# Gate logits out of the value projection, one value product over four query blocks, and a new order for the five stages

## The chip, the cores and the metric

One core of a Trainium2 chip runs the whole program. The metric is device time in microseconds, lower is better: the median of 3 runs before is 1630.82 us (1628.48 to 1631.11). Engines by their short names: PE multiplies matrices (PEld is its weight load), DVE and ACT work on vectors, POOL is the slow general engine, SP only issues DMAs.

## The reference

Three residual layers on a sequence of 512 tokens, width 1024, in fp32. First a gated delta-rule mixer (8 heads of 128, in chunks, with a triangular solve) and a SwiGLU FFN (2816 wide); then a forgetting attention and a second FFN; then a block with two attentions side by side (a sparse one, "A", that keeps 128 keys per query chosen by an indexer, and a dense one, "B", causal in chunks of 64). What the change touches:

```python
def shared_kv(x, kv_norm, w_kv, b_forget):
    kvf = rms_norm(x, kv_norm) @ w_kv              # 1024 x (1024 keys, 1024 values, 16 gates)
    ...
    f_logit = kvf[..., 2 * FOX_WIDTH:] + b_forget  # one gate logit per token and head
    log_f_cum = jnp.cumsum(jax.nn.log_sigmoid(f_logit), axis=1).transpose(0, 2, 1)
    return k, v, log_f_cum

def forgetting_attention_mixer(h, w_q, w_o, k, v, log_f_cum):
    for blk in range(t_len // 128):                # four query blocks, keys up to their own end
        s = q_blk @ k[:e].T * scale + log_f_cum[q] - log_f_cum[keys]
        p = softmax(where(mask, s, -inf))
        outs.append(p @ v[:e])
    return concat(outs) @ w_o
```

## The kernel before, in words

Activations lie transposed: 8 tiles of 128 features x 512 tokens. Every fp32 operand of a large product is split into a high and a low part (`fp32r`), and a product is three matmuls, high x high, high x low, low x high (`mm3`). Weights come by DMA on SP, 128 x 1024 at a time; the high part is a cast on ACT or DVE, the low part is a second cast of the negated high part, to which a DMA on POOL adds the weight again, or a subtraction on DVE or POOL (`lows`, `weight`).

`fm_tile` makes one output tile of 128 features x 512 tokens (weights stand, activations move, 24 matmuls of 512 columns); `tm_group` makes a token-major product: 4 banks, one per block of 128 tokens, n weight columns moving, weight units of 128 x 1024 in turn. The value projection of the forgetting attention ("fox") is two such groups of 512 columns, 8 heads each (`values_of`).

The forget gates' logits come from `small_proj`: 16 columns, high and low parts side by side in a stationary tile padded with zeros, 16 matmuls of 512 columns, then transposed to tokens; then the log-sigmoid as a chain of small DVE steps, a scan over tokens on DVE, and transposes back. The first scores need its result (`gates`, `cq`).

`attend` is one head of any of the three attentions. For each of four query blocks: scores into a bank, softmax on DVE and ACT, transposition on PE, then the transposed probabilities are copied to their high part and subtracted into the low part. Two query blocks share one pair of tiles; as soon as both are there, each key block's values (high and low side by side, stationary) meet the high and the low part: 4 and 8 matmuls for the two pairs of query blocks.

The output projection of a mixer is halved over its input: `out_half` multiplies the first four of eight head pairs while the other heads still run; `out_proj` adds the second four, for tokens 0 to 255 and then 256 to 511, so that the norm after it (`add_normed`) starts on the first half.

The order of instructions is not that of the code. `Program.record` lists operations; `schedule` replays them on a model of the engines' queues and issues whatever can start first, the lowest key among equals. `SHIFTS` move the keys of large products back, `SELECT_SHIFT`, `SUMS_SHIFT`, `START_SHIFT` those of some other work; `WINDOWS` say how far ahead of the oldest open operation it may go; `DEAR` sets what it adds to an engine's end when an operation may go on several engines; `cost`, `timed`, `lag` and `LATE` are its durations and delays. `GDN_ORDER`, `FOX_ORDER` and `B2_ORDER` are the order in which the parts are listed: in fox V are value groups, K key projections, H a pair of heads, O the first half of the output projection; in the last block S are the selections of A (a chain of DVE maxima), B and A head pairs.

In the first stage (`gdn`), `inverses` solves four heads' triangular blocks together: blocks go through DRAM to 64 partitions, 30 dependent pairs of DVE steps follow, and the result goes back through DRAM; `doubled` then finishes it with chains of small products and copies.

Of the kernel before, what the change touches and what calls it, by code (L numbers as in the profile page):

```python
# [16 lines left out]
T = 512  # L17
NT = 4
# [23 lines left out]
SUMS_SHIFT = 53  # L42
START_SHIFT = 133
# [3 lines left out]
MARGIN, LATE, SLOW = 100, 400, 1.04  # L47
# [126 lines left out]
class Program:  # L174
# [166 lines left out]
    def schedule(self):  # L341
# [27 lines left out]
        def ready(i):  # L369
# [214 lines left out]
class Net:  # L584
# [154 lines left out]
    def fm_tile(self, out, w, xs, cols=FULL):  # L739

        nk = len(xs)
        with self.later(self.shift):
            for k in range(nk):
                a = (w[0][:, k * 128:(k + 1) * 128], w[1][:, k * 128:(k + 1) * 128])
                b = (xs[k][0][:, cols], xs[k][1][:, cols])
                self.mm3(out, a, b, k == 0, k == nk - 1)
# [124 lines left out]
    def out_proj(self, w, o, f, x, post, pre, dst):  # L871
# [14 lines left out]
    def run(self):  # L886
# [7 lines left out]
        for layer, (mix, nxt, w) in enumerate((("gdn", "fox", "gdn_w_out"), ("fox", "b2", "fox_w_o"))):  # L894
# [8 lines left out]
            with self.after(f[0]) if mix in st else nullcontext():  # L903
                x = self.loaded(src)
# [179 lines left out]
    def gdn(self, y, w_out):  # L1084
# [82 lines left out]
        def conv_silu(m, ps):  # L1167
# [7 lines left out]
            th, s = self.t(), self.t()  # L1175
# [35 lines left out]
        def keys(h):  # L1211
            s = conv_silu(8 + h, proj(8 + h))
# [6 lines left out]
            kds[h] = self.t()  # L1219
# [164 lines left out]
        for step in GDN_ORDER.split():  # L1384
# [11 lines left out]
            else:  # L1396
                f = self.out_half(w_out, [out[h] for h in range(G4)])
# [54 lines left out]
    def attend(self, passes, bias, vhl, out, row=None):  # L1452
# [4 lines left out]
        po = self.bank()  # L1457
        for p in range(2):
            ph, pl = (self.t(512 * (p + 1), F32R) for _ in range(2))
            for j in range(2):  # L1460
# [21 lines left out]
                src = pt.rearrange("p (k q) -> p k q", q=128)  # L1482
                dh, dl = (t.rearrange("p (k j q) -> p k j q", j=2, q=128)[:, :qb + 1, j] for t in (ph, pl))
                self.copy(dh, src)
                V.tensor_sub(dl, src, dh.bitcast(F32))
            last = 2 * p + 1
            for kb in range(last + 1):
# [3 lines left out]
                PE.matmul(po[:, q], vhl(kb), pl[:, c], start=False, stop=(kb == last))  # L1491
        lo = self.t(T)
# [11 lines left out]
    def fox(self, y, x, w_out):  # L1504
# [11 lines left out]
        f = self.small_proj(d["w_f"], H, xs)  # L1516
        tokens = lambda: self.t(NT * H).rearrange("p (n h) -> p n h", n=NT)
        ps, ls, w2, c, z = self.bank(), tokens(), tokens(), self.t(p=H), self.t(p=H)
        for n in range(NT):
            PE.transpose(ps[:, n * H:(n + 1) * H], f[:, n * 128:(n + 1) * 128], self.ident[0:H, 0:H])  # L1520
        V.tensor_tensor(ls, ps[:, :NT * H].rearrange("p (n h) -> p n h", n=NT),
                        y.rc[:, :, None].to_broadcast([128, NT, H]), op=OP.mult)
        V.tensor_tensor(ls, ls, bf[:, None, :].to_broadcast([128, NT, H]), op=OP.add)
        self.log1p_exp_neg_abs(w2, ls, tokens)
        V.scalar_tensor_tensor(ls, ls, 0.0, w2, op0=OP.min, op1=OP.subtract)
        ps = self.bank()
        for n in range(NT):
            PE.transpose(ps[0:H, n * 128:(n + 1) * 128], ls[:, n], self.ident)
        V.memset(z, 0.0)
        V.tensor_tensor_scan(c, ps[0:H], z, 0.0, op0=OP.add, op1=OP.add)  # L1530
        cq = self.t(NT * H)
        ps = self.bank()
        for n in range(NT):
            PE.transpose(ps[:, n * H:(n + 1) * H], c[:, n * 128:(n + 1) * 128], self.ident[0:H, 0:H])
        V.tensor_copy(cq, ps[:, :NT * H])

        gates = self.t(T, F32R, p=48)
        V.memset(gates.bitcast(F32), 0.0)
        self.split(gates[0:H], gates[32:32 + H], c, -1.0)


        vt = [self.value_tiles() for _ in range(2)]
# [479 lines left out]
```

## Time and profile before

| | before |
|---|---|
| median of 3 runs | 1630.82 us |
| profiled execution | 1631.0 us, span 1629.3 us |
| PE busy | 1599.5 us, 98% |
| PE weight loads busy | 1422.7 us, 87% |
| DVE busy | 1293.1 us, 79% |
| ACT busy | 1056.7 us, 65% |
| POOL busy | 477.8 us, 29% |
| read from memory | 258 MB |

The span runs from the first to the last instruction; a little of the execution lies around it. PE's busy time counts matmuls by modelled ends, and neighbours overlap, so what a matmul costs in a stream is the distance between starts. Nearly all instructions carry one line (552, where the planner issues them), so groups are told by tile: `wide` are tiles of 1024 columns (weights, values, probabilities), `big` of 512, `s` small ones, `psum` the banks. In a PE row the moving operand stands first, the stationary one second.

### The profile page before, as it was taken

Reading aid. Unit: us, or ns where it says so; the run is one execution under the profiler, and the core shown is the slowest. Engines: PE = TensorE matmul, PEld = TensorE weight load, DVE = VectorE, ACT = ScalarE, POOL = GpSimd, SP = SyncE. Lnnn points to the kernel's source line nnn. Section 1 sums busy time; section 2 is a strip of 40 time slices with the busy share of each in tenths; the row PEclk is TensorE's granted clock in tenths of the full one; section 3 lists DMA queues with packets and bytes.
Section 4 is the critical chain, followed back from the end, with each engine's and each line's share of the span. In section 5 each row is a group of like instructions: output and inputs, shape, how many; then the busy total and the mean of one; then the engine's idle time right before and its main releaser. Section 6 shows DMA issues by size and latency. Waiting matters only on the chain.

```text
span 1629.3 us, 28818 instructions
## 1 busy us (share of the span) xinstructions
PE 1599.5 (98%) x10184; PEld 1422.7 (87%) x10184; DVE 1293.1 (79%) x3055; ACT 1056.7 (65%) x2096; POOL 477.8 (29%) x490
## 2 busy tenths in 40 slices
PE   8999999999999999999999999999999999999998
PEld 6888888998998989888878999999989889888777
DVE  7976986799785848686969699776858669999795
ACT  8716645585654635556869686655646679796794
POOL 2502411223331433213343123322315222304610
PEclk9998999999999999999999999999999999999999
DMA  9837448367796887974355757896969983439722
GB/s 289 232 53 189 115 85 243 95 153 183 189 239 142 217 170 194 282 195 123 92 117 119 181 143 186 188 231 153 228 149 259 253 195 63 130 98 208 184 56 65
DMA packets 114512, 272.31 MB, mean 167 GB/s; under 512 B 25240, under 2 KB 30104, under 8 KB 114368
## 3 DMA queue, kind: packets, MB, share of 16 engines
q0 software_dynamic: 38128, 108.05, 37.9%
q1 hardware_dynamic: 76240, 162.42, 30.1%
q8 instruction: 80, 1.31, 0.3%
q14 instruction: 64, 0.52, 0.1%
HBM read 258.29 MB, written 12.08 MB: 166 GB/s over the span
## 4 chain that ended last, share of the span: by engine, by line
PE 79%; DVE 10%; ACT 4%; DMA 2%; issue 2%; POOL 1%; SPq 0%; DVEq 0%; POOLq 0%; ACTq 0%
PE psum L552 79%; DVE big L552 8%; ACT big L552 2%; DVE wide L552 2%; ACT wide L552 2%; DMA wide<-in_w_ffn_in_dram 1%; DVE s L552 1%; DMA big<-scratch_rows 0%; SPq L552 0%; POOL big L552 0%; ACT s L552 0%; DMA wide<-in_w_gdn_dram 0%; DMA big<-in_xT_dram 0%; DMA scratch_blocks_t<-wide 0%; POOL wide L552 0%
## 5 line engine op out<-in xcount | busy, mean ns | idle before, releaser
L552 PE MATMUL psum<-big,wide 128*128 128x256 f32 (+1 forms) x7264 | 1224.8, 325 | 14.4 <-ACT big L552 8.5
L552 PEld LDWEIGHTS psum<-big,wide 128*128 128x128 f32 x7264 | 1036.8, 189 | 124.1 <-ACT big L552 10.2
L552 DVE TENSOR_TENSOR big<-psum,big 128x256 f32<-128x256 f32 (+5 forms) x550 | 254.9, 477 | 145.6 <-PE psum L552 135.3
L552 ACT CAST wide<-wide 128x1024 fp32r<-128x1024 f32 (+4 forms) x303 | 281.0, 940 | 114.1 <-PE psum L552 67.6
L552 ACT ACTIVATE big<-big 128x256 f32<-128x256 f32 (+4 forms) x335 | 170.6, 523 | 135.8 <-DVE big L552 130.1
L552 ACT ACTIVATE wide<-wide 128x1024 fp32r<-128x1024 f32 (+4 forms) x217 | 193.7, 901 | 72.4 <-PE psum L552 53.8
L552 DVE TENSOR_TENSOR big<-big,big 128x256 f32<-128x256 f32 (+3 forms) x391 | 221.4, 581 | 21.4 <-ACT big L552 17.5
L552 PE MATMUL psum<-wide,big 128*128 128x512 f32 (+2 forms) x924 | 206.5, 372 | 1.6 <-ACT big L552 1.6
L552 DVE TENSOR_TENSOR wide<-wide,wide 128x512 f32<-128x512 f32 (+2 forms) x181 | 175.4, 976 | 33.3 <-PE psum L552 28.6
L552 PEld LDWEIGHTS psum<-wide,big 128*128 128x128 f32 x924 | 157.8, 188 | 29.7 <-ACT big L552 2.0
L552 ACT COPY big<-psum 128x512 f32<-128x512 f32 (+7 forms) x188 | 84.1, 456 | 119.0 <-PE psum L552 117.0
L552 POOL DMA_DIRECT2D wide<-in_w_ffn_in_dram x88 | 78.5, 896 | 226.6 <-ACT wide L552 196.9
L552 ACT ACTIVATE big<-big,s 128x256 f32<-128x256 f32 (+3 forms) x227 | 119.9, 557 | 10.6 <-DVE s L552 10.2
L552 DVE SCALAR_TENSOR_TENSOR big<-big,big 128x512 f32<-128x512 f32 (+3 forms) x153 | 111.0, 728 | 15.5 <-ACT big L552 11.7
L552 POOL TENSOR_TENSOR s<-s,half 128x4 f32<-128x4 f32 (+2 forms) x50 | 64.3, 1286 | 187.0 <-DVE s L552 186.9
L552 PE MATMUL psum<-big,big 128*128 128x128 f32 (+13 forms) x672 | 111.8, 297 | 4.0 <-DVE big L552 1.7
L552 PEld LDWEIGHTS psum<-big,big 128*128 128x128 f32 (+6 forms) x672 | 88.1, 183 | 13.9 <-DVE big L552 2.6
L552 PE MATMUL psum<-ident,big 128*128 128x128 f32 (+2 forms) x564 | 93.4, 273 | 4.1 <-DVE big L552 1.7
L552 POOL DMA_DIRECT2D wide<-in_w_ffn_out_dram x64 | 56.6, 899 | 135.5 <-ACT wide L552 125.9
L552 POOL TENSOR_TENSOR wide<-wide,wide 128x512 f32<-128x512 f32 (+1 forms) x40 | 68.4, 1709 | 74.0 <-DVE wide L552 26.7
L552 PEld LDWEIGHTS psum<-ident,big 128*128 128x128 f32 (+2 forms) x564 | 67.3, 141 | 19.5 <-DVE big L552 3.4
L552 POOL TENSOR_TENSOR big<-big,big 64x512 fp32r<-64x512 f32 (+3 forms) x44 | 55.4, 1264 | 86.1 <-ACT big L552 43.7
(131 smaller groups left out, 1383.3 us busy)
## 6 DMA issues: line engine op xcount, KB each, us to landing
wide<-in_w_ffn_in_dram SPq DMA_DIRECT2D x88, 512.0 KB
wide<-in_w_ffn_in_dram POOLq DMA_DIRECT2D x48, 512.0 KB, 5.8
wide<-in_w_gdn_dram SPq DMA_DIRECT2D x31, 512.0 KB
wide<-in_w_ffn_out_dram SPq DMA_DIRECT2D x32, 384.0 KB
wide<-in_w_ffn_out_dram POOLq DMA_DIRECT2D x32, 384.0 KB, 7.4
wide<-in_w_gdn_dram POOLq DMA_DIRECT2D x22, 512.0 KB, 7.7
wide<-in_w_ffn_in_dram POOLq DMA_DIRECT2D x40, 256.0 KB, 6.1
wide<-in_w_ffn_out_dram SPq DMA_DIRECT2D x32, 320.0 KB
```

Of the source, the lines that this page charges most:

```text
L552: getattr(eng[o.eng], fn)(*(real(a) for a in args), **{k: real(a) for k, a in kw.items()})
```

## The change

- **Gates.** `small_proj` and its transposes are gone from fox (gdn keeps its own). The values' weights are packed as three groups of 5, 5 and 6 heads (`VALUES`), and the gates' 16 columns stand behind the first group's 320. V0's evacuation writes the logits by token, scaled, with the bias. `forget`, the same chain as before, follows V0 in the list.
- **Value products.** With `joint`, `attend` waits for all four query blocks; the probabilities of a key block then lie side by side in one of two tile pairs, and each key block has one matmul over all query blocks that see it, for each part: 512, 384, 256 and 128 columns. `JOINT` turns it on in fox and in A, not in B.
- **Late half.** With `LATE_OUT` = 2 in fox, the last four of eight output tiles get only tokens 0 to 255 in `out_half`; the other 256 are accumulated in `out_proj` ahead of the second half's own terms, with the weights loaded once more. In gdn it is 0.
- **Order.** Constants of the planner, three lists, and four of its prices change.
- `WIDE_KEYS` is empty, so the keys' tiles of gdn stay as they are.

```diff
-SHIFTS = {"gdn": 103, "ffn0": 286, "fox": 0, "ffn1": 95, "b2": 261}
-DEAR = {"gdn": {"DVE": 1050, "ACT": -450, "POOL": 1350},
-        "ffn0": {"DVE": 1200, "ACT": -350, "POOL": 1250},
-        "fox": {"DVE": 450, "ACT": -200, "POOL": 1000},
-        "ffn1": {"DVE": 1700, "ACT": -100, "POOL": 1800},
-        "b2": {"DVE": 450, "ACT": -300, "POOL": 600}}
-WINDOWS = {"gdn": 861, "ffn0": 1118, "fox": 2257, "ffn1": 762, "b2": 938}
-GDN_ORDER = ("K1 K2 K0 K3 P0 P2 I0 K4 D0 P1 D1 R0 R1 D3 P3 R3 K7 D2 K5 K6 I1 R2 P5 O0 D4 D5 D7 "
+SHIFTS = {"gdn": 121, "ffn0": 321, "fox": 21, "ffn1": 87, "b2": 278}
+DEAR = {"gdn": {"DVE": 1050, "ACT": -350, "POOL": 1350},
+        "ffn0": {"DVE": 850, "ACT": 150, "POOL": 1500},
+        "fox": {"DVE": 450, "ACT": 0, "POOL": 1000},
+        "ffn1": {"DVE": 1900, "ACT": -100, "POOL": 1600},
+        "b2": {"DVE": 550, "ACT": -500, "POOL": 550}}
+WINDOWS = {"gdn": 861, "ffn0": 885, "fox": 810, "ffn1": 930, "b2": 978}
+GDN_ORDER = ("K1 K2 K0 K3 P0 P2 I0 K4 D0 P1 D1 R0 R1 D3 P3 R3 K7 D2 K5 K6 I1 D5 R2 P5 O0 D4 D7 "
              "D6 P7 P4 P6 R4 R5 R7 R6")
-FOX_ORDER = "V0 K012 K4 H2 K6 H1 K3 H3 K7 H0 V1 H6 K5 H4 H7 H5 O"
-B2_ORDER = "B1 B3 S3 B2 S2 S1 B0 v k q o A1 A0 A2 A3"
-SELECT_SHIFT = 1156
-SUMS_SHIFT = 53
-START_SHIFT = 133
+VALUES = (0, 5, 10, 16)
+FOX_ORDER = "K012 V0 K4 V1 H2 K6 H1 K3 K7 H3 H0 V2 H6 K5 H4 H7 H5 O"
+B2_ORDER = "B1 B3 B0 S3 B2 S2 v k q S1 o A1 A0 A2 A3"
+SELECT_SHIFT = 1314
+JOINT = (True, False, True)
+LATE_OUT = (0, 2)
+SUMS_SHIFT = 50
+START_SHIFT = 226
-MARGIN, LATE, SLOW = 100, 400, 1.04
+MARGIN, LATE, SLOW = 100, 200, 1.04
...
         dur, size = self.cost(eng, fn, args, kw)
+        if not size and eng != "PE" and args[0].shape[0] <= 64 and dur > 300:
+            dur += 90
...
             if args[1].dt == F32R:
-                return 2.5 + max(0.8 * m, n / 2.25), 0
+                return 4.2 + max(0.8 * m, n / 2.25), 0
...
                 if q == "POOL" and o.size:
-                    o.est[q] += 220
+                    o.est[q] += 400
...
-    def out_half(self, w, o):
+    def out_half(self, w, o, late):
         f = [self.t() for _ in range(KD)]
-        self.half_product(w, o, slice(0, 512), lambda m, ps: self.copy(f[m], ps))
-        return f
+        first = KD - 2 * late
+        for m in range(0, KD, 2):
+            cols = FULL if m < first else HALVES[0]
+            for i, parts in enumerate(self.weight_pair(w, m, slice(0, 512))):
+                bank = self.bank()[:, :cols.stop]
+                self.fm_tile(bank, parts, o, cols)
+                self.copy(f[m + i][:, cols], bank)
+        return f, o, first
...
+        w4 = sum((self.weight_pair(w, m, slice(0, 512)) for m in range(first, KD, 2)), [])
         for cols in HALVES:
             acc = self.t(256)
             for m in range(KD):
                 bank = self.bank()[:, :256]
-                self.fm_tile(bank, ws[m], o, cols)
-                self.V.tensor_add(f[m][:, cols], bank, f[m][:, cols])
+                if m >= first and cols is HALVES[1]:
+                    self.fm_tile(bank, w4[m - first], o4, cols, stop=False)
+                    self.fm_tile(bank, ws[m], o, cols, start=False)
+                    self.copy(f[m][:, cols], bank)
+                else:
+                    self.fm_tile(bank, ws[m], o, cols)
+                    self.V.tensor_add(f[m][:, cols], bank, f[m][:, cols])
...
                 src = pt.rearrange("p (k q) -> p k q", q=128)
+                if joint:
+                    for a, b in ((0, min(qb + 1, 2)), (2, qb + 1)):
+                        if a < b:
...
+                            self.copy(dh, src[:, a:b])
+                            V.tensor_sub(dl, src[:, a:b], dh.bitcast(F32))
+                    continue
...
+        if joint:
+            for kb in range(NT):
+                q, c = slice(kb * 128, 512), slice((0, 512, 0, 256)[kb], (512, 896, 256, 384)[kb])
+                for part in (ph, pl):
+                    PE.matmul(po[:, q], vhl(kb), part[kb // 2][:, c], start=(kb == 0 and part is ph),
+                              stop=(kb == NT - 1 and part is pl))
...
-        f = self.small_proj(d["w_f"], H, xs)
...
+        def values_of(i):
+            def evac(tb, ps):
...
+                if i == 0:
+                    V.scalar_tensor_tensor(ls[:, tb], ps[:, n - H:], y.rc[:, tb:tb + 1], bf, op0=OP.mult, op1=OP.add)
+            n = (VALUES[i + 1] - VALUES[i]) * 64 + (H if i == 0 else 0)
+            self.tm_group([d[f"w_v{i}"][j] for j in range(4)], n, xs, evac)
...
+                if step == "V0":
+                    forget()
```

## Rows read from the trace of the kernel before

**Rows 1.** The page: busy us (share), instructions; granted clock in 40 slices.
```profile
PE 1599.5 (98%) x10184; PEld 1422.7 (87%) x10184; DVE 1293.1 (79%) x3055; ACT 1056.7 (65%) x2096; POOL 477.8 (29%) x490
...
PEclk9998999999999999999999999999999999999999
```

**Rows 2.** PE in order of time: start us, us, operation, out<-in, count.
```profile
689.67 7.12 PE L552 MATMUL psum<-wide,big 128*128 128x512 f32 x30
696.62 0.50 PE L552 MATMUL psum<-ones,big 128*128 128x1 f32 x4
...
894.67 0.92 PE L552 MATMUL psum<-wide,wide 128*128 128x256 f32 x7
895.43 0.30 PE L552 MATMUL psum<-ident,big 128*128 128x128 f32 x1
...
952.58 14.05 PE L552 MATMUL psum<-big,wide 128*128 128x256 f32 x117
966.47 0.50 PE L552 MATMUL psum<-ones,big 128*128 128x1 f32 x4
```

**Rows 3.** Windows: us, busy us (x) by PE, PEld, DVE, ACT, POOL; clock, DMA.
```profile
750.00:840.00 90.00, 89.91 (x495) 75.84 (x495) 70.59 (x244) 70.76 (x167) 31.37 (x32) 1.00 0.45 106
840.00:900.00 60.00, 57.18 (x330) 47.09 (x329) 57.78 (x227) 54.73 (x136) 20.80 (x17) 1.00 0.44 105
1540.00:1612.00 72.00, 68.59 (x404) 57.03 (x404) 65.90 (x183) 61.81 (x155) 15.84 (x12) 1.00 0.25 49
```

**Rows 4.** DVE groups by shape, windows 840 to 900 and 1540 to 1612: softmax rows.
```profile
L552 DVE CUSTOM_DVE_ANT_0 big<-psum,big 128x512 f32<-128x512 f32 x8 | 5.4, 676 | 0.0
...
L552 DVE CUSTOM_DVE_ANT_0 big<-psum,big 128x512 f32<-128x512 f32 x8 | 5.4, 679 | 0.0
```

**Rows 5.** PE and ACT in order of time [idle before], and windows, near the first inverse.
```profile
126.96 0.69 PE L552 MATMUL psum<-ident,big 128*128 128x128 f32 x2 [1.23 <-ACT big L552]
...
122.89 0.37 ACT L552 COPY big<-psum 96x256 f32<-96x256 f32 x1 [31.81 <-PE psum L552]
...
122.00:129.00 7.00, 4.89 (x40) 4.01 (x40) 4.60 (x7) 5.05 (x10) 0.57 (x1) 0.73 0.99 331
129.00:139.00 10.00, 9.62 (x55) 9.37 (x55) 5.35 (x12) 4.57 (x18) 3.48 (x4) 0.51 0.73 146
```

**Rows 6.** PE in order of time, at the start of ffn1.
```profile
973.10 2.79 PE L552 MATMUL psum<-big,wide 128*128 128x256 f32 x19 [0.63 <-DVE big L552]
976.99 13.23 PE L552 MATMUL psum<-big,wide 128*128 128x256 f32 x104 [1.09 <-ACT big L552]
```

**Rows 7.** PE in order of time: the gates' logits turned, the first scores.
```profile
719.22 0.42 PE L552 MATMUL psum<-ident,big 16*128 16x16 f32 x4
...
747.91 2.06 PE L552 MATMUL psum<-big,big 66*128 66x128 f32 x12
```

**Rows 8.** Groups by shape, whole span: busy us, mean ns | idle before us.
```profile
L552 DVE TENSOR_TENSOR wide<-psum,wide 128x512 fp32r<-128x512 f32 x32 | 22.0, 687 | 3.8 <-ACT wide L552 3.2
L552 DVE TENSOR_TENSOR wide<-psum,wide 128x384 fp32r<-128x384 f32 x32 | 17.6, 549 | 1.1 <-PE psum L552 0.5 <-ACT wide L552 0.2
L552 DVE TENSOR_TENSOR big<-psum,big 128x256 fp32r<-128x256 f32 x32 | 13.3, 417 | 0.3
L552 DVE TENSOR_TENSOR big<-psum,big 128x128 fp32r<-128x128 f32 x32 | 9.0, 283 | 0.2
...
L552 ACT CAST wide<-wide 128x1024 fp32r<-128x1024 f32 x203 | 210.4, 1046 | 78.6 <-PE psum L552 49.5 <-DVE wide L552 19.3 <-issue 6.5
L552 ACT CAST wide<-psum 128x512 fp32r<-128x512 f32 x30 | 17.3, 578 | 2.9 <-PE psum L552 2.8
L552 ACT CAST wide<-psum 128x384 fp32r<-128x384 f32 x31 | 14.8, 477 | 0.9 <-PE psum L552 0.6
L552 ACT CAST big<-psum 128x256 fp32r<-128x256 f32 x31 | 11.4, 366 | 0.1
L552 ACT CAST big<-psum 128x128 fp32r<-128x128 f32 x29 | 7.6, 262 | 0.3
```

More of the change, by code (lines that the diff above doesn't have):

```diff
@@ L736, in weight_pair, with fm_tile @@
         return [(hi[:, c], lo[:, c]) for c in (slice(0, 512), slice(512, 1024))]
-    def fm_tile(self, out, w, xs, cols=FULL):
+    def fm_tile(self, out, w, xs, cols=FULL, start=True, stop=True):
         nk = len(xs)
@@ L745, in fm_tile @@
                 b = (xs[k][0][:, cols], xs[k][1][:, cols])
-                self.mm3(out, a, b, k == 0, k == nk - 1)
+                self.mm3(out, a, b, start and k == 0, stop and k == nk - 1)
     def fm_phase(self, items, nk_cols, xs, evac, head=False, tail=False):
@@ L902, in run @@
             dst = d[f"x{layer}"] if nxt in st else d["out"]
-            with self.after(f[0]) if mix in st else nullcontext():
+            with self.after(f[0][0]) if mix in st else nullcontext():
                 x = self.loaded(src)
@@ L1211, in keys @@
         def keys(h):
-            s = conv_silu(8 + h, proj(8 + h))
+            both = self.t(1024) if h in WIDE_KEYS else None
+            s = conv_silu(8 + h, proj(8 + h), None if both is None else both[:, :512])
             ps = turned(s)
@@ L1396, in gdn @@
             else:
-                f = self.out_half(w_out, [out[h] for h in range(G4)])
+                f = self.out_half(w_out, [out[h] for h in range(G4)], LATE_OUT[0])
         return [out[h] for h in range(G4, H)], f
@@ L1450, in value_tiles, with attend @@
         return [self.t(1024, F32R).rearrange("p (h c) -> p h c", c=128) for _ in range(NT)]
-    def attend(self, passes, bias, vhl, out, row=None):
+    def attend(self, passes, bias, vhl, out, row=None, joint=False):
         V, A, PE = self.V, self.A, self.PE
         po = self.bank()
+        if joint:
+            ph, pl = ((self.t(1024, F32R), self.t(384, F32R)) for _ in range(2))
         for p in range(2):
-            ph, pl = (self.t(512 * (p + 1), F32R) for _ in range(2))
+            if not joint:
+                ph, pl = (self.t(512 * (p + 1), F32R) for _ in range(2))
             for j in range(2):
@@ L1485, in attend @@
                 V.tensor_sub(dl, src, dh.bitcast(F32))
+            if joint:
+                continue
             last = 2 * p + 1
@@ L1514, in fox @@
                         fill=NEG, base=0, channel_multiplier=1)
-        f = self.small_proj(d["w_f"], H, xs)
+        vt = [self.value_tiles() for _ in range(2)]
         tokens = lambda: self.t(NT * H).rearrange("p (n h) -> p n h", n=NT)
[L1518 to L1542, printed above, removed]
-        def values_of(half):
-            self.tm_group([d["w_v"][4 * half + i] for i in range(4)], 512, xs,
-                          lambda tb, ps: self.values(vt[half][tb], ps.rearrange("p (h c) -> p h c", c=64),
-                                                     y.rc[:, tb:tb + 1]))
+        ls, cq, gates = tokens(), self.t(NT * H), self.t(T, F32R, p=48)
@@ new lines, in values_of @@
+        def values_of(i):
+            def evac(tb, ps):
+                for half in range(2):
+                    lo, hi = max(VALUES[i], 8 * half), min(VALUES[i + 1], 8 * half + 8)
+                    if lo < hi:
+                        src = ps[:, (lo - VALUES[i]) * 64:(hi - VALUES[i]) * 64]
+                        self.values(vt[half][tb][:, lo - 8 * half:hi - 8 * half],
+                                    src.rearrange("p (h c) -> p h c", c=64), y.rc[:, tb:tb + 1])
+                if i == 0:
+                    V.scalar_tensor_tensor(ls[:, tb], ps[:, n - H:], y.rc[:, tb:tb + 1], bf, op0=OP.mult, op1=OP.add)
+            n = (VALUES[i + 1] - VALUES[i]) * 64 + (H if i == 0 else 0)
+            self.tm_group([d[f"w_v{i}"][j] for j in range(4)], n, xs, evac)
@@ new lines, in forget @@
+        def forget():
+            w2, c, z = tokens(), self.t(p=H), self.t(p=H)
+            self.log1p_exp_neg_abs(w2, ls, tokens)
+            V.scalar_tensor_tensor(ls, ls, 0.0, w2, op0=OP.min, op1=OP.subtract)
+            ps = self.bank()
+            for n in range(NT):
+                PE.transpose(ps[0:H, n * 128:(n + 1) * 128], ls[:, n], self.ident)
+            V.memset(z, 0.0)
+            V.tensor_tensor_scan(c, ps[0:H], z, 0.0, op0=OP.add, op1=OP.add)
+            ps = self.bank()
+            for n in range(NT):
+                PE.transpose(ps[:, n * H:(n + 1) * H], c[:, n * 128:(n + 1) * 128], self.ident[0:H, 0:H])
+            V.tensor_copy(cq, ps[:, :NT * H])
+            V.memset(gates.bitcast(F32), 0.0)
+            self.split(gates[0:H], gates[32:32 + H], c, -1.0)
@@ L1602, in fox @@
             else:
-                f = self.out_half(w_out, self.parts([o.pop(m) for m in range(4)]))
+                f = self.out_half(w_out, self.parts([o.pop(m) for m in range(4)]), LATE_OUT[1])
         return self.parts([o[m] for m in range(4, KD)]), f
@@ L1954, in pack @@
     out["w_k"] = pack_fm(w[:, :1024])
-    out["w_v"] = pack_tm(w[:, 1024:2048], 512)
-    out["w_f"] = np.ascontiguousarray(w[:, 2048:].reshape(KD, 128, 16).transpose(1, 0, 2))
+    for n in range(3):
+        cols = w[:, 1024 + 64 * VALUES[n]:1024 + 64 * VALUES[n + 1]]
+        if n == 0:
+            cols = np.concatenate([cols, w[:, 2048:]], 1)
+        out[f"w_v{n}"] = pack_tm(cols, cols.shape[1])
     out["b_forget"] = i["b_forget"].reshape(1, 16)
```

21 lines of the change are left out of this document (14 added, 7 removed).

## The prediction

> **What bounds the kernel now.** I read the page first: busy time by engine, then the slices and the granted clock. PE is busy for 1599.5 of 1629.3 us and its clock row is full but for the fourth slice [rows 1]. So nearly every microsecond is PE's, and an edit counts by how much PE work it takes away and by what it does to the few places where PE stands. Next I read PE in order of time, to price a matmul by the distance from one group's start to the next (the printed durations overlap). 30 matmuls of 512 columns take 696.62 - 689.67 = 6.95 us, 231.7 ns each; 117 of 256 columns take 966.47 - 952.58 = 13.89 us, 118.7 ns each; the seven last of a value product, five of 256 and two of 128 columns, take 895.43 - 894.67 = 0.76 us, so (760 - 5 x 118.7) / 2 = 83 ns for 128 columns [rows 2]. Halving 256 columns thus saves only a third. The places where PE stands come from the windows. In 840 to 900 us PE idles 2.8 us while DVE is 57.78 of 60 busy and ACT 54.73; in 1540 to 1612 PE idles 3.4 us with DVE at 65.90 and ACT at 61.81 of 72 [rows 3]. These are the stretches of the attention heads: the softmax rows of 512 columns count eight of fox's sixteen in the first and all eight of attention A in the second [rows 4]. The third place is the first triangular inverse, near 122 us: PE waits 1.23 us among small products, ACT has stood for 31.81 us, and the clock, full before, averages 0.73 in 122 to 129 and 0.51 in 129 to 139, so PE is at the lower level, 1.2 GHz [rows 5]. The fourth is the start of ffn1, with waits of 0.63 and 1.09 us [rows 6].
>
> **Part 1, the gates' logits.** Removed: the separate projection, 16 matmuls of 512 columns and 4 small transposes: 16 x 231.7 = 3.71 us, and 0.42 us [rows 2, 7]. Changed: the value projections were 2 groups x 96 matmuls of 512 columns and become 3 groups x 96 of 336 (16 of them the gates), 320 and 384 columns. No row has these widths; on the line between 118.7 and 231.7 ns (0.441 ns a column) they cost 154.0, 146.9 and 175.2. Before 192 x 231.7 = 44.49 us, after 96 x 476.1 = 45.71: +1.22. Sum of part 1: -3.71 - 0.42 + 1.22 = -2.91 us, all on PE, in a stretch where PE is the bound. Its bounds: 1040 columns at the 512's own 0.4525 ns each cost 96 x 470.6 = 45.18, +0.69, so -3.44; at the 256's 0.4637 ns, 46.29, +1.80, so -2.33. The weights now come in 12 units instead of 8: 4 more SP and POOL issues, and 4 more pairs of casts, which are narrower each; I cost them at nothing, since ACT is 70.76 of 90 us busy while PE has no gap [rows 3]; uncovered, four pairs of casts at 1.05 us each [rows 8] would be 8.4 us of ACT, less what the narrower ones give back. The wait that is added: the log-sigmoid chain now follows the last unit of V0, which stands behind K0 to K2. DVE's small operations queue behind it, and the first scores wait for its end. Before, the logits were turned at 719.22 and the first scores ran at 747.91 [rows 7], 29 us that PE filled with projections; after, K4 and V1 stand in that gap. I take 0, with up to 4 us if V0 drains late.
>
> **Part 2, one value product over four query blocks.** It applies to fox (16 heads) and attention A (8), not to B. A head had 8 matmuls of 256 and 4 of 128 columns: 8 x 118.7 + 4 x 83 = 1282 ns. It gets two each of 512, 384, 256 and 128: 2 x (231.7 + 175.2 + 118.7 + 83) = 1217 ns. The columns are the same, 2560; what goes is 4 matmuls, 65 ns a head, 1.6 us for 24 heads. On the other side the transposed probabilities now lie in two tiles, so that query blocks 2 and 3 are copied and subtracted in two pieces. DVE: 549 becomes 417 + 283, 687 becomes 2 x 417, +298 ns a head; the copies, nearly all on ACT: 477 becomes 366 + 262, 578 becomes 2 x 366, +305 ns [rows 8]. For 24 heads that is 7.2 us of DVE and 7.3 of ACT. Where PE is the bound it is free. In the two stretches of [rows 3] DVE is the bound: 8 x 0.298 = 2.4 us each. I take it as exposed in A, where all heads lie in one stretch and nothing stands behind, and as hidden in fox, where heads can start into the emptier 750 to 840 us (DVE 70.59 of 90). Part 2: -1.6 + 2.4 = +0.8 us, between -1.6 (all hidden) and -1.6 + 16 x 0.603 = +8.0 (both engines exposed one after the other in both).
>
> The Trainium skill's page "TensorE: Matmul & The Clock Gate", section "Back-to-back issue gap", gives columns over 2.4 GHz and 2.5 ns for a matmul alone, so 55.8 ns for 128 columns, and 81 ns measured where each brings its weight load. By the first a head would go from 1097 to 1087 ns and this part would save PE 0.24 us instead of 1.6, which speaks against it (the whole sum would be 1625.2); the trace, with 83 ns [rows 2], agrees with the second.
>
> **Part 3, the late half of fox's output projection.** Four of its eight output tiles are computed in the first pass for the first 256 tokens only; the other 256 are made later, in the bank of the second pass. 48 matmuls of 512 become 96 of 256: 48 x (237.4 - 231.7) = +0.27 us. What moves is 48 x 118.7 = 5.7 us of PE work, from ahead of the first half's products to between the halves. So the norm of the first half starts up to 5.7 us earlier and PE comes that much later to the products that wait for it: the waits of 0.63 and 1.09 us [rows 6] should go, -1.72. What is late next is DVE, which makes the FFN's sums there. Two weight pairs are loaded a second time: 2 issues on SP, 2 on POOL, 4 casts of 1.05 us [rows 8], beside a PE that has work; 4.2 us of ACT if it had not. Part 3: +0.27 - 1.72 = -1.45 us, from +4.5 to -1.45.
>
> **Part 4, the order.** The planner's shifts, prices, windows and orders change everywhere, so every queue is dealt anew, SP's and POOL's too. Nothing is removed by it; it can only win back what [rows 3, 5, 6] show as lost, or lose more. Steps of at most 64 partitions are priced 90 ns higher when they are long, which touches the widest steps of the inverse; DMAs are thought to land earlier on one count and to be issued later on POOL. The largest piece is the cold stretch: by [rows 5] PE is at half clock for 7 x 0.27 / 0.5 + 10 x 0.49 / 0.5 = 13.6 us, which do the work of 6.8. A projection that falls between the small products would cover it; but DVE still runs the whole inverse by itself and PE's banks fill meanwhile, which the change leaves as it is. Between 0 and -6.8 - 1.2 (PE's wait there) I take half of the cold price, -3.4. That is a choice, the softest number here.
>
> **Sum.** The profiled execution took 1631.0 us: 1629.3 of span and 1.7 around it, 0.2 over the median of the runs. -2.91 + 0.8 - 1.45 - 3.4 = -7.0, so 1624.0, and 1623.8 against the median, which I give; the rivals' times are also against the median.
>
> **Rivals.**
> 1. The order wins much more. The cold stretch goes with its wait (-8.0), and half of the 6.2 us of PE idle in the two head stretches goes (-3.1): -2.91 + 0.8 - 1.45 - 8.0 - 3.1 = -14.7, 1616.1. For it: what PE loses lies in few places, which an order can reach. Against: DVE is full in two of them and gets more to do.
> 2. Slower: the evacuations of part 2 take over. Place: the two head stretches. Price: 16 heads x 0.603 us = 9.6, with the cold stretch and ffn1's waits kept: -2.91 - 1.6 + 9.6 + 0.27 = +5.4, 1636.2. It decides where DVE and ACT together pass what the heads' stretch has to spare: 2.2 and 5.3 us of 60 in fox, 6.1 and 10.2 of 72 in A [rows 3], against 2.4 of each per stretch. It needs fox's heads to be bunched as now. V2 is smaller than the old V1 (96 x 175.2 = 16.8 us against 22.2) and 5.7 us of output products leave too, so there is less cover between heads: that speaks for it.
> 3. Nothing to be measured: cold stretch and waits stay or only move: -2.91 + 0.8 + 0.27 = -1.8, 1629.0; with the gates' chain late by 4 us, 1633.
> 4. A new cold stretch somewhere, at the price of the one there is, 6.8 us: -2.91 + 0.8 - 1.45 + 6.8 = +3.2, 1634.0.
>
> **Chances.** Forecast 0.45 (own range 1617 to 1628), rival 1 0.20, rival 2 0.14, rival 3 0.15, rival 4 0.06. A measurement of this kernel tells about 0.2% (3.3 us) from no change, so faster is below 1627.5 and slower above 1634.1. Faster: 0.41 + 0.20 + 0.03 = 0.64. Same: 0.04 + 0.11 + 0.02 + 0.02 = 0.19. Slower: 0.12 + 0.01 + 0.04 = 0.17. The range that leaves 0.2 out goes from 1611, below the first rival, to 1636, the second.
>
> **What would show it.** Part 1: no 16-row transposes in the fox stage, 96 matmuls each of 336, 320 and 384 columns at 154, 147 and 175 ns; first scores no later than 750 us from the span's start. Part 2: six copies and six subtractions a head, none over 256 columns; PE's value products at 1.22 us a head; DVE's share in A's stretch at 95% or more and the stretch 2.4 us longer than its 72. Part 3: no PE wait of over 0.3 us at ffn1's start. Part 4: the clock row full, or a shorter stretch of 0.5 near 130 us. The prediction is wrong if PE's busy time falls by less than 3 us, or if the head stretches show PE idle over 10 us, or if more than 5 us come from places that no part names.

## The result, and the profile after

The changed kernel takes 1648.18 us (median of 4 runs, 1640.99 to 1651.51) beside 1630.21 of the kernel before on the same chip: ratio 1.0107, 95% interval 1.0087 to 1.0126. It is slower; the forecast was 1623.8 and the range ended at 1636. The profiled execution took 1648.7 us, its span 1647.0.

The page after, busy time of PE and the clock, as in [rows 1]:

```profile
PE 1600.4 (97%) x10212; PEld 1431.5 (87%) x10212; DVE 1296.8 (79%) x3101; ACT 1057.9 (64%) x2153; POOL 510.8 (31%) x513
...
PEclk9998999999999999999999999999998999999999
```

PE is as busy as before although it has less to do, and the clock row has a second notch, in the 31st slice (1235 to 1276 us). To see which stage lost, I use the small matmuls with `ones`, which close each norm and so mark the stage borders. PE in order of time, the last mark of gdn, ffn0 and ffn1 before (fox's, at 966.47, is in [rows 2]), then of all four after:

```profile
358.75 0.50 PE L552 MATMUL psum<-ones,big 128*128 128x1 f32 x4
...
679.08 0.50 PE L552 MATMUL psum<-ones,big 128*128 128x1 f32 x4
...
1286.01 0.50 PE L552 MATMUL psum<-ones,big 128*128 128x1 f32 x4
```

```profile
364.08 0.50 PE L558 MATMUL psum<-ones,big 128*128 128x1 f32 x4
...
685.28 0.50 PE L558 MATMUL psum<-ones,big 128*128 128x1 f32 x4
...
969.24 0.50 PE L558 MATMUL psum<-ones,big 128*128 128x1 f32 x4
...
1307.26 0.50 PE L558 MATMUL psum<-ones,big 128*128 128x1 f32 x4
```

The distances between marks give the stages, here for all kernels that compute the whole layer (same marks in each trace, us; the runs are described below):

| stage | before | after | e1a | e1b | e1c | e4 | e3a | e3b | e6 | e9a | e9b |
|---|---|---|---|---|---|---|---|---|---|---|---|
| gdn | 358.8 | 364.1 | 362.3 | 364.1 | 361.2 | 362.2 | 357.3 | 362.7 | 356.6 | 359.3 | 357.9 |
| ffn0 | 320.3 | 321.2 | 321.2 | 321.2 | 321.2 | 321.2 | 319.8 | 321.2 | 319.9 | 320.6 | 320.0 |
| fox | 287.4 | 284.0 | 285.5 | 284.3 | 283.6 | 287.2 | 306.5 | 295.1 | 283.2 | 285.1 | 288.0 |
| ffn1 | 319.5 | 338.0 | 326.5 | 321.6 | 319.5 | 324.1 | 322.3 | 334.3 | 321.4 | 319.6 | 318.9 |
| block 2 | 343.3 | 339.8 | 339.4 | 339.6 | 339.4 | 339.5 | 341.0 | 340.0 | 339.3 | 339.8 | 338.9 |
| span | 1629.3 | 1647.0 | 1634.9 | 1630.8 | 1624.8 | 1634.2 | 1646.9 | 1653.3 | 1620.5 | 1624.5 | 1623.8 |

Fox and block 2, where the parts lie, each got some 3.5 us shorter. ffn1, inside which no part lies, got 18.5 longer, and gdn 5.3. The loss in ffn1 lies at its end. Windows of 1220 to 1264 us, before and after, columns as in [rows 3]:

```profile
1220.00:1264.00 44.00, 44.00 (x371) 43.87 (x371) 37.75 (x62) 27.58 (x41) 21.05 (x27) 1.00 0.95 252
```

```profile
1220.00:1264.00 44.00, 32.32 (x236) 31.91 (x235) 30.53 (x31) 15.91 (x23) 22.49 (x22) 0.84 0.65 161
```

PE idles 11.7 of 44 us and the clock averages 0.84, so part of it ran at 1.2 GHz. The two add up to the loss: 11.7 us of standing and, by the clock, some 7 us of lost speed. PE in order of time names what it waited for. Of this kind of wait, for a `wide` tile from DVE, the whole trace of before has one, 1.1 us at 890 us in fox, and that of after three, 12.2 us, of which these two are 11.7:

```profile
1236.10 11.14 PE L558 MATMUL psum<-big,wide 128*128 128x256 f32 x79 [3.82 <-DVE wide L558]
1255.11 15.16 PE L558 MATMUL psum<-big,wide 128*128 128x256 f32 x104 [7.86 <-DVE wide L558]
```

Both wait for a weight's low part, which DVE makes by a subtraction of two tiles in SBUF, the memory on the chip. DVE and POOL in order of time, around the second:

```profile
1247.30 7.76 DVE L558 TENSOR_TENSOR wide<-wide,wide 128x1024 fp32r<-128x1024 f32 x1
1254.98 0.68 DVE L558 TENSOR_TENSOR big<-big,big 128x512 f32<-128x512 f32 x1
```

```profile
1247.07 0.88 POOL L558 DMA_DIRECT2D wide<-in_w_ffn_in_dram  x1 [2.65 <-PE psum L558]
1247.69 5.06 POOL L558 TENSOR_TENSOR wide<-wide,wide 128x512 f32<-128x512 f32 x3
1252.43 1.53 POOL L558 TENSOR_TENSOR wide<-wide 128x512 f32<-128x512 f32 x1
```

The subtraction takes 7.76 us. Over the trace the same shape with no POOL arithmetic beside it takes 1.22 (at most 1.23). It starts 0.39 us ahead of POOL's four instructions and ends 1.1 us after the last: it stood until the whole train (the run of POOL instructions back to back) was through. Three DVE instructions before it, at 1228.82, 1232.21 and 1241.59, take 3.4 to 3.8 us; each starts while POOL issues a DMA and ends 0.6 to 1.1 us after the one POOL sum that follows that DMA.

### The profile page after: what moved, and what is told of

Same layout as the page of the kernel before. It is cut to its first block, busy times and chain, and to the rows that moved or that the text cites. A ratio compares the mean times of both kernels' runs of the same rounds, so it can differ in the third digit from the quotient of the medians.

```text
span 1647.0 us, 29102 instructions
## 1 busy us (share of the span) xinstructions
PE 1600.4 (97%) x10212; PEld 1431.5 (87%) x10212; DVE 1296.8 (79%) x3101; ACT 1057.9 (64%) x2153; POOL 510.8 (31%) x513
## 4 chain that ended last, share of the span: by engine, by line
PE 73%; DVE 12%; ACT 6%; issue 4%; DMA 3%; POOL 2%; SPq 0%; POOLq 0%; ACTq 0%; DVEq 0%
PE psum L558 73%; DVE big L558 8%; ACT big L558 4%; DVE wide L558 2%; ACT wide L558 2%; DVE s L558 2%; POOL big L558 1%; DMA big<-scratch_x 1%; POOL s L558 0%; DMA wide<-in_w_ffn_out_dram 0%; DMA wide<-in_w_va_dram 0%; POOL wide L558 0%; DMA big<-scratch_rows 0%; DMA big<-in_xT_dram 0%; DMA scratch_x<-big 0%
## 5 line engine op out<-in xcount | busy, mean ns | idle before, releaser
L558 PE MATMUL psum<-big,wide 128*128 128x256 f32 (+2 forms) x7296 | 1227.5, 325 | 26.3 <-DVE wide L558 11.7
L558 ACT ACTIVATE big<-big 128x256 f32<-128x256 f32 (+4 forms) x335 | 170.3, 523 | 151.7 <-DVE big L558 148.2
L558 DVE TENSOR_TENSOR big<-big,big 128x256 f32<-128x256 f32 (+3 forms) x382 | 207.6, 559 | 21.9 <-ACT big L558 18.1
L558 DVE TENSOR_TENSOR wide<-wide,wide 128x512 f32<-128x512 f32 (+2 forms) x183 | 184.3, 1015 | 50.5 <-PE psum L558 37.3
L558 PE MATMUL psum<-wide,big 128*128 128x512 f32 (+5 forms) x1020 | 211.2, 355 | 0.6 <-DMA wide<-in_w_va_dram 0.3
L558 PEld LDWEIGHTS psum<-wide,big 128*128 128x128 f32 x1020 | 168.0, 188 | 22.5 <-DMA wide<-in_w_va_dram 0.8
L558 ACT COPY big<-psum 128x256 f32<-128x256 f32 (+8 forms) x182 | 79.6, 447 | 125.8 <-PE psum L558 123.8
L558 ACT ACTIVATE big<-big,s 128x384 f32<-128x384 f32 (+3 forms) x233 | 122.7, 560 | 11.3 <-DVE s L558 9.7
L558 PE MATMUL psum<-big,big 128*128 128x128 f32 (+14 forms) x672 | 109.3, 296 | 3.9 <-DVE big L558 1.3
L558 POOL TENSOR_TENSOR big<-big,big 64x512 fp32r<-64x512 f32 (+3 forms) x53 | 66.7, 1275 | 121.6 <-DVE big L558 48.1
L558 POOL TENSOR_TENSOR wide<-wide,wide 128x512 f32<-128x512 f32 (+2 forms) x39 | 71.4, 1848 | 54.6 <-PE psum L558 27.8
```

The lines of the kernel that those rows point to most:

```text
L558: getattr(eng[o.eng], fn)(*(real(a) for a in args), **{k: real(a) for k, a in kw.items()})
```

## The experiments

**Theory A (port).** DVE and POOL share a way into SBUF, a port. The order gave POOL a train of sums at the end of ffn1; DVE's instructions with two SBUF operands stand beside it (the pile), PE runs out of weights, and the clock falls. **Rival B.** One of the parts costs the time, or the evacuations of the joint product do. **Rival C.** The stages are just longer everywhere, and the pile is a symptom of being late.

### Sums taken off POOL, order kept (e1a, e1b, e1c)

```diff
+            pool = -1
             for _, i in self.order:
                 o = self.ops[i]
+                pool += o.eng == "POOL"
+                if o.eng == "POOL" and pool in MOVED:
+                    o.eng = "DVE"
```

e1a has `MOVED` = 382 to 385, the four of the train, e1b 374, 376, 377 and 380 too, e1c also 30, 33, 210, 281, 282 and 347.

> The changed kernel, issue order kept; the four POOL sums that stand beside the 7.76 us DVE subtraction at 1247 us go to DVE at their place in the order. Port theory (a DVE instruction with two SBUF operands stands until POOL's train of elementwise instructions ends; that made the loss at the end of ffn1): PE's wait of 7.86 us goes and with it the cold stretch of 10.24 us behind it, worth half: 7.9 + 5.1 = 13 us, so 1635 us. Rival, the parts themselves (evacuations, more weight units) cost it: 1648 us, moved by under 2. Rival, a late DMA holds DVE there: the subtraction stays at over 5 us, 1648 us.

Measured: 1637.58 us, ratio 1.0047 (1.0028 to 1.0066): 10.6 us back of the 13 expected. The same subtraction now takes 1.22 us; three instructions of 3.0 to 3.8 us are still there.

> The same with the eight POOL elementwise instructions between 1229 and 1254 us on DVE. Port theory: also the wait of 3.82 us and the cold stretch of 3.4 us behind it go, 5.5 us more: 1630 us (1628 to 1633), and the runs lie within 4 us instead of 10, since the collision hangs on tenths of a microsecond. Parts theory: 1648 us and the same spread. Late DMA: 1648 us.

Measured: 1631.90 us, ratio 1.0013 (1.0003 to 1.0022). DVE got eight instructions more, and yet 16 us came back: ffn1 is at 321.6, and in the stretch PE has no gap and the full clock:

```profile
1236.00:1264.00 28.00, 28.00 (x240) 28.00 (x239) 24.91 (x45) 15.70 (x25) 8.62 (x11) 1.00 0.98 257
```

As the cause of these 16 us, POOL's sums beside DVE hold, and B and C fall: all parts and the other stages are as in the changed kernel. That it is a port that they share is not shown by it.

> The changed kernel with its order kept and fourteen of GpSimd's elementwise instructions given to VectorE: the eight of the last experiment and six that stood beside VectorE instructions of 1.8 to 2.9 us at 69, 75, 734, 973 and 1156 us. Port theory: another 2 to 4 us under 1631.9: 1629 (1626 to 1631). Rival, these stalls are covered or the added VectorE work eats them: 1632 to 1634.

Measured: 1628.31 us, ratio 0.9994 (0.9984 to 1.0004). That is 3.6 us less than e1b (3.1 by the ratios, as the two ran on different chips): the same rule wins a little in other stretches too. ffn1 is at 319.5 now, as before the change.

### Parts and order apart (e3a, e3b, e4)

e3a is the changed kernel with the planner's constants, lists and prices of the kernel before, e3b the kernel before with the new ones (the edits in short):

```diff
 # e3a: after, with
+SHIFTS, DEAR, WINDOWS, GDN_ORDER, B2_ORDER, prices   # as before
+FOX_ORDER = "V0 V1 K012 K4 H2 K6 H1 K3 H3 K7 H0 V2 H6 K5 H4 H7 H5 O"
 # e3b: before, with
+SHIFTS, DEAR, WINDOWS, GDN_ORDER, B2_ORDER, prices   # as after
+FOX_ORDER = "K012 V0 K4 H2 K6 H1 K3 K7 H3 H0 V1 H6 K5 H4 H7 H5 O"
```

> The three parts (gates in V0, joint products, late half) with the constants, lists and prices of the kernel before (FOX list: V0 V1 first, V2 where V1 stood). Port theory: PE's work falls by the 4.2 us as in the changed kernel and no DVE instruction stands over 5 us: 1626 us, give or take 6 for a new plan. Parts theory: 1640 us or more. If the order in general carries luck of 10 us and more, anything from 1615 to 1645.

Measured: 1649.15 us, ratio 1.0120 (1.0105 to 1.0135): a miss. ffn1 has no pile, but fox takes 306.5 us. Windows 680 to 840 us of the kernel before and of e3a:

```profile
680.00:840.00 160.00, 157.51 (x894) 134.42 (x893) 124.14 (x379) 113.35 (x244) 47.54 (x49) 1.00 0.60 150
```

```profile
680.00:840.00 160.00, 147.38 (x875) 130.27 (x874) 123.77 (x399) 108.88 (x256) 37.53 (x38) 0.98 0.52 135
```

PE idles 10 us more, spread over waits for ACT, DVE and DMAs of weights. With fox's old constants and this list the parts lose 19 us; the old order is no cure for fox.

> The kernel before with the new constants, lists and prices, without the three parts. If the loss belongs to the order: 1640 us or more, with DVE instructions standing over 3 us beside POOL trains. If it belongs to the parts: 1630 us. Port theory makes no claim on the size, only that the trace shows PE waiting behind such DVE instructions where it is slower.

Measured: 1657.87 us, ratio 1.0176 (1.0159 to 1.0193). Without any part the pile is back, with a DVE instruction of the same 7.76 us:

```profile
1254.45 7.76 DVE L558 TENSOR_TENSOR wide<-wide,wide 128x1024 fp32r<-128x1024 f32 x1
```

```profile
1262.27 13.01 PE L558 MATMUL psum<-big,wide 128*128 128x256 f32 x96 [7.55 <-DVE wide L558]
```

The pile is the order's. Fox shows something else beside it: the new order alone makes it 7.7 us longer, the parts alone (e3a) 19.1, both together 3.4 shorter. Parts and order don't add up there; with these lists each was good only with the other. In block 2 the new order alone already gives 340.0 us, where the kernel before has 343.3. Which lines of the order make the pile:

```diff
 # e4: after, with
-SHIFTS["ffn1"], WINDOWS["ffn1"] = 87, 930
+SHIFTS["ffn1"], WINDOWS["ffn1"] = 95, 762
-DEAR["ffn1"] = {"DVE": 1900, "ACT": -100, "POOL": 1600}
+DEAR["ffn1"] = {"DVE": 1700, "ACT": -100, "POOL": 1800}
```

> The changed kernel with the three planner constants of ffn1 (shift, prices of the engines, window) as in the kernel before; parts and all else as changed. Order theory (the loss is the GpSimd train at ffn1's end, which these constants decide): no VectorE instruction over 3 us near 1230 to 1250, no cold stretch there, 16 us back: 1632 (1628 to 1637). Rival, the parts or the prices of steps make the train: the pile stays, 1645 to 1650.

Measured: 1634.82 us, ratio 1.0030 (1.0017 to 1.0044). ffn1 falls by 13.9 us, from 338.0 to 324.1, and fox is 3.2 longer. POOL has 33 instructions of arithmetic in ffn1 before, 52 after and 37 in e4. The new prices made DVE 200 ns dearer and POOL 200 cheaper, which fits; shift and window were set back with them, so the prices by themselves are not shown to have dealt the train to POOL.

### The port by itself (p1 to p3)

Small kernels without the layer; in each round ACT releases a DVE subtraction of 128x1024 and a train of POOL additions of 128x512 (the code in short):

```diff
+A.copy(b[:, 0:8], k[:, 0:8])                  # releases POOL's train
+A.copy(a[:, 0:late], k[:, 0:late])            # releases DVE
+P.dma_start(l, src, accum_op=OP.add)          # cases with a DMA ahead (l written just before)
+for i in range(train):
+    P.tensor_tensor(e[i], b[:, 0:512], k[:, 512:1024], op=OP.add)
+V.tensor_tensor(c, a, k, op=OP.subtract)
```

> No part of the layer is computed: ten small cases of one VectorE tensor_tensor of 128x1024 with both operands in SBUF (in "halves" two of 128x512) beside none, one, two or four GpSimd tensor_tensors of 128x512 back to back, all released by ScalarE. Train theory (the VectorE instruction stands until the whole train of GpSimd is through): alone 1.22 us; beside one GpSimd instruction of about 0.7 us some 1.9; beside two 2.6; beside four 4.0 or more, also where the train is released half a microsecond after VectorE ("fourlate") if the 7.76 us instruction at 1247.30 is the rule. Rival, turns (the port changes hands after each instruction): never more than about 2 us, whatever the train, and the two halves each wait for one GpSimd instruction. Second rival, the queue's own DMA: only the case with a DMA issued on GpSimd ahead of the train shows over 3 us.

Measured: the train theory in this form is wrong. A DVE instruction that comes first takes its 1.23 us whatever the train ("four"), and one that comes 0.41 us into a running train waits for one POOL instruction (1.26 us alone; "dvelate"), then has its turn:

```profile
82.15 1.23 DVE L51 TENSOR_TENSOR four_c<-four_a,k 128x1024 f32<-128x1024 f32 x1 [5.49 <-ACT four_a L41]
...
223.28 1.93 DVE L51 TENSOR_TENSOR dvelate_c<-dvelate_a,k 128x1024 f32<-128x1024 f32 x1 [4.67 <-ACT dvelate_a L45]
```

> No part of the layer is computed: a VectorE tensor_tensor of two SBUF operands (1024 columns, in "h4w8" 512) is released just after GpSimd starts, which issues a DMA ("d" cases) and then a train of 0, 1, 2 or 4 tensor_tensors of 128x512, all ready. In the first study VectorE came ahead of the DMA and was never slowed (1.23 us), and beside a running train it waited for one instruction (1.93 us). DMA theory: a VectorE instruction that starts while GpSimd issues a DMA, with elementwise instructions queued behind it, stands until the last of these is through: 1.2 + 1.3 a GpSimd instruction, so about 2.5, 3.8 and 6.5 us for d1, d2 and d4; without a train (d0) 1.2; without a DMA (t4) 1.9 to 2.4; released by a copy of 1024 columns (about 1 us later, in the train) like t4 or like d4. Rival, back to back: what counts is that VectorE was at work just before ("b4", "bt4"), with or without the DMA; then only these two are over 3 us. If none is over 3 us, neither is the cause of the 7.76 us.

Measured: in most cases DVE started between 0.2 us ahead of the DMA's issue and 0.05 into it and was not slowed (1.23 us), so d0 to d2 say nothing. Where it started 0.26 us into the issue it took 3.02, and 0.7 into it 2.59; with DVE at work just before it started 0.13 into it and took 3.13, without the DMA 2.10. That is one POOL instruction and the rest of the issue, still not four. What d0 leaves open the changed kernel's trace has: 29 DVE subtractions or sums of 512 columns started during the issue of a POOL DMA with no POOL arithmetic beside them, and none took over 0.69 us.

> No part of the layer is computed. In the first two studies all of GpSimd's instructions of a train wrote one tile, so each waited for the one before and left a gap of some 80 ns; in the kernel they write tiles of their own and overlap. Here VectorE's 1024 columns come about 0.4 us into a train of 1, 2 or 4 GpSimd instructions of 128x512 that write one tile ("same") or their own ("own"), without and with a DMA ahead ("d"). Gap theory: with a gap VectorE gets its turn after one instruction (same 1.9 us, dsame 3.0); without one it stands until the train is through, 1.2 + 1.25 for each GpSimd instruction less the 0.4: own1 about 2, own2 about 3.3, own 5.5, down 6 to 7. Rival, gaps don't matter: own as same, 1.9, and the 7.76 us instruction stays unexplained.

Measured, DVE and then POOL of the last case ("own" also names the shorter trains, which took the same 1.93):

```profile
14.00 1.94 DVE L46 TENSOR_TENSOR same_c<-same_a,k 128x1024 f32<-128x1024 f32 x1 [4.68 <-ACT same_a L41]
...
42.56 1.93 DVE L46 TENSOR_TENSOR own_c<-own_a,k 128x1024 f32<-128x1024 f32 x1 [4.44 <-ACT own_a L41]
...
103.78 3.02 DVE L46 TENSOR_TENSOR dsame_c<-dsame_a,k 128x1024 f32<-128x1024 f32 x1 [6.25 <-ACT dsame_a L41]
...
138.66 6.64 DVE L46 TENSOR_TENSOR down_c<-down_a,k 128x1024 f32<-128x1024 f32 x1 [2.06 <-ACT down_a L41]
```

```profile
138.41 0.88 POOL L43 DMA_DIRECT2D down_l<-in_x_dram  x1 [2.90 <-ACT down_l L40]
139.01 1.56 POOL L45 TENSOR_TENSOR down_ep<-down_b,k 128x512 f32<-128x512 f32 x1
140.24 1.55 POOL L45 TENSOR_TENSOR down_eq<-down_b,k 128x512 f32<-128x512 f32 x1
141.46 1.55 POOL L45 TENSOR_TENSOR down_er<-down_b,k 128x512 f32<-128x512 f32 x1
142.68 1.54 POOL L45 TENSOR_TENSOR down_es<-down_b,k 128x512 f32<-128x512 f32 x1
```

Half of the gap theory fell (own as same), half held ("dsame" took 3.02 in three of its four rounds and 1.23 in the first). In these small kernels it takes two things at once: DVE starts while POOL issues a DMA, and the POOL instructions behind it don't wait for each other. Then DVE stands until the last is through, 6.64 us for 1.23. This is the picture of 1247 us: DMA at 1247.07, DVE at 1247.30, four independent sums. Behind a DMA the sums start 0.33 us before the one ahead ends (1.55 long, 1.22 apart); without it they overlap by 0.04 (1.26 and 1.22). That this overlap is what keeps DVE out was not tried by itself, and the two conditions need not be exact: the kernel before has a DVE instruction of 3.07 us (shown below) that started 0.2 us after the issue had ended.

### The old order where no part is (e6, e9a, e9b)

```diff
 # e6: after, with gdn, ffn0 and ffn1 planned as before
+OLD = ("gdn", "ffn0", "ffn1")   # their SHIFTS, DEAR, WINDOWS, lists, and the prices of their steps
 # e9a: e6 with
-JOINT = (True, False, True)
+JOINT = (False, False, False)
 # e9b: e6 with
-LATE_OUT = (0, 2)
+LATE_OUT = (0, 0)
```

> The changed kernel with gdn, ffn0 and ffn1 planned as before (their constants, lists and prices of steps), fox and b2 with the parts and the order of the change. If the parts are worth what their matmuls say (4.35 us of PE) and the first stages' new order loses 6 us against the old, as the excess over the matmuls' own time by stretch shows, the sum is the kernel before less 4 us: 1626 (1622 to 1630). Rival, a stage's order is good only behind the order that it was searched with: fox and b2 lose some 10 us again, 1635 or more.

Measured: 1622.98 us, ratio 0.9962 (0.9947 to 0.9977). It beats both kernels. The page of e6 has PE busy for 9.4 us less than before; 4.3 of it is the parts' work, as counted below:

```profile
PE 1590.1 (98%) x10212; PEld 1423.2 (88%) x10212; DVE 1300.9 (80%) x3114; ACT 1060.4 (65%) x2154; POOL 485.9 (30%) x499
```

> The combination of old order in gdn and the FFNs with the three parts (1622.98), value products back to two per head (planned anew). If part 2 costs as forecast, -1.6 of PE and +2.4 of exposed evacuations, it gets 0.8 faster without: 1622. If the evacuations are hidden, it gets 1.6 slower: 1624.6. Measured PE work (matmuls by their own median times) up by 1.6 in both. A step of over 3 us either way is the planner's new order, not the part.

Measured: 1625.79 us, ratio 0.9970 (0.9959 to 0.9981).

> The same combination with the whole first pass of fox's output projection at once (planned anew). Forecast of part 3: 1.45 of gain, so 1624.4 without it and longer PE waits at the start of ffn1. If the waits there are the port's (a VectorE instruction beside GpSimd's), they stay as they are with or without the part and only its 0.27 us of PE comes back: 1622.7.

Measured: 1625.45 us, ratio 0.9975 (0.9964 to 0.9987). Both intervals overlap that of e6, so a part's own worth isn't told apart by the times; the stages of the table say more, below.

## Why the prediction was wrong

**PE's work (parts 1 to 3): right.** Count every matmul at the median distance of starts of its shape over all traces (232.0 ns for 512 columns, 176.0, 154.0 and 146.5 for 384, 336 and 320, 118.0 for 256, 87 for a value product's 128) and PE has 1572.6 us before and 1568.3 after: -4.3, forecast -2.91 - 1.6 + 0.27 = -4.24. The interpolated widths came within 0.8 ns. Without the joint product (e9a) the count is 1.6 us higher, as forecast. PE's busy time, which was to show it by falling 3 us, rose by 0.9: matmuls at 1.2 GHz count longer (those of 256 columns start 213 ns apart from 1255 to 1261 us after, where the clock was 0.5), so it was a bad sign to name. Two of its other signs did show the miss: the clock row has a second notch, and over 5 us came from a place that no part names, the end of ffn1.

**Gates' chain: late by little.** Before, fox had two groups of 16-row transposes, one that turned the logits to tokens (719.22, [rows 7]) and one that turns the result of the scan; here that second one in the kernel before, then, in the changed kernel, the one that is left and the first scores:

```profile
733.26 0.42 PE L552 MATMUL psum<-ident,big 16*128 16x16 f32 x4
```

```profile
743.25 0.42 PE L558 MATMUL psum<-ident,big 16*128 16x16 f32 x4
...
757.09 1.82 PE L558 MATMUL psum<-big,big 66*128 66x128 f32 x11
```

So the 0.42 us of part 1 are gone, though its sign, no such transposes in fox, was worded too widely. The first scores came at 747.91 before [rows 7]. Counted from the end of ffn0 they come at 71.8 us now and came at 68.8 before; the "no later than 750" was missed by 7.1, of which 6.2 came from the stages ahead. Fox got shorter all the same.

**Evacuations, +2.4 in A: not there.** Block 2 got 3.5 us shorter. Windows after, each with its eight softmax rows of 512 columns, against [rows 3]:

```profile
845.00:905.00 60.00, 58.37 (x318) 48.13 (x318) 57.71 (x244) 55.97 (x145) 24.32 (x20) 1.00 0.56 170
1560.00:1632.00 72.00, 71.44 (x397) 59.99 (x396) 63.22 (x194) 66.30 (x180) 19.82 (x15) 1.00 0.28 52
```

PE idles 1.6 and 0.6 us where it idled 2.8 and 3.4. The order changed with the parts, so the comparison that counts is e9a, without the joint product, against e6: 339.8 us in block 2 against 339.3. The 8 x 65 ns of PE come back and no evacuation shows in the stage, and in fox e9a is 1.9 us longer, not shorter. Rival 2 is refuted with it. A's softmax rows of 512, first to last, do lie further apart with it, 50.5 us in e6 and 46.5 in e9a, so the heads may have got slower; the block did not. DVE's share of 92% in [rows 3] was not a bound.

**Part 3's waits, -1.72: wrong.** At the start of ffn1 after, against [rows 6]:

```profile
975.55 0.62 PE L558 MATMUL psum<-big,wide 128*128 128x256 f32 x3 [1.46 <-DVE big L558]
976.56 13.61 PE L558 MATMUL psum<-big,wide 128*128 128x256 f32 x100 [0.39 <-DVE big L558]
```

1.85 us beside 1.72. What ends last is DVE's 512-column instruction, with POOL's DMA at 972.59 and sums at 973.22 and 973.92 beside it:

```profile
973.25 2.24 DVE L558 TENSOR_TENSOR big<-big,big 128x512 fp32r<-128x512 f32 x1
```

It is the same collision: in e1c, which takes these two sums off POOL, this DVE instruction takes 0.68 us and only the wait of 0.39 is left. What the part does show is a shift: without it (e9b against e6, both planned anew) fox is 4.8 us longer and ffn1 2.5 shorter, 2.3 in the part's favour where 1.45 were forecast; by the times of the runs that is not told from nothing, and it did not come from these waits.

**Part 4, the order, -3.4: the step that failed.** The text said that the order "can only win back what [rows 3, 5, 6] show as lost, or lose more", and then priced only the gain. It measured +6.2 to the end of ffn0 and +18.5 in ffn1, 24.7 us, more than the whole miss of 24.4. Rival 4, a new cold stretch, had the kind right and 0.06 of the chance, and 6.8 us for what became 16: it counted the clock and not PE's standing that precedes it. The row that could have warned is in the trace of before, beside POOL's products and behind its DMA:

```profile
1226.94 3.07 DVE L552 TENSOR_TENSOR big<-big,big 128x512 f32<-128x512 f32 x1
```

PE didn't wait for it there, so it cost nothing yet. POOL made cheaper and DVE dearer in just that stage was in the diff.

The piece that part 4 hoped for, the cold stretch at the first inverse, was not won: the changed kernel has it from 134.5 to 148.2 us at a mean clock of 0.50, as long as before. And it changes with the order left as it is. Up to 300 us e6, e9a and e9b issue the same 2764 instructions of PE, DVE, ACT and POOL in the same order on each engine as the kernel before; windows 120 to 145 us of before, e6 and e9a:

```profile
120.00:145.00 25.00, 22.48 (x147) 20.07 (x146) 13.16 (x23) 13.82 (x34) 6.25 (x6) 0.73 0.68 168
```

```profile
120.00:145.00 25.00, 22.25 (x161) 19.69 (x160) 14.72 (x27) 15.54 (x36) 7.46 (x8) 0.86 0.77 189
```

```profile
120.00:145.00 25.00, 21.16 (x146) 19.05 (x145) 13.17 (x23) 13.65 (x33) 6.24 (x6) 0.80 0.68 170
```

The granted clock differs from execution to execution, 0.73 to 0.86, by the windows worth 3.3 us; the ends of gdn differ by 2.7 between these kernels, and not in step with it. So half of what the cold stretch costs comes and goes without any change of order. Whether another order could remove it was not tried.

**What stays open.** Why the new order is 5 us worse in gdn: it ends at 362.2 to 364.1 us in five kernels with that order there (after, e1a, e1b, e3b, e4) and at 356.6 to 359.3 in five with the old one. PE stands 2.3 us from 60 to 80 us in the changed kernel (nothing before), which e1c brings to 0.2, so that part is POOL's sums again, though e1c has 0.7 more right behind it; and 2.9 us from 145 to 200 us (0.6 before), in waits among small products that no run explains. Open too is which of fox's constants makes e3a lose 19 us there.

The Trainium skill's page "SBUF — State Buffer", section "Who interferes with whom", says that a VectorE (DVE) instruction with two SBUF inputs contends with a GpSimd (POOL) one that reads SBUF, that what they share is an exclusive lock, and that the order of issue decides who blocks. The measured 1.93 us, the rest of one POOL instruction and then DVE's own time, and the 1.23 us of the DVE instruction that came first agree; the 6.64 and 7.76 us don't, where DVE started ahead of all four and came last.

## What to carry to other kernels

Price a new order from both sides: look up the longest instruction that a shared resource has already made in the old trace, and what an order that deals more work to that resource would do with it. By these traces, keep independent POOL sums from following a POOL DMA where DVE has two operands in SBUF at that moment; moving eight sums to the busier engine won 16 us. And when parts and order change together, keep the old order for the stages that the parts don't touch, and try each without the other: the first turned 1648 into 1623 here, the second showed that in fox each alone lost.

## What had not been expected of the hardware

A DVE instruction of 1.23 us took 6.64 to 7.76 behind a POOL DMA and four independent POOL sums, 1.93 to 2.10 behind the sums alone, 3.02 behind a DMA and sums that wait for each other. And the same instructions in the same order met a granted clock of 0.73, 0.80 or 0.86 in the same 25 us.
